# Low halves of weight blocks on GpSimd outside the recurrences, and new durations in the planner's table

## The chip, the cores and the metric

One NeuronCore of a Trainium2 chip runs the whole program. It has a matrix engine (TensorE, PE in the profile, with its weight loads as PEld), three engines for elementwise work (VectorE, DVE; ScalarE, ACT; GpSimd, POOL), a queue that issues transfers (SyncE, SP), an on-chip memory (SBUF, 128 partitions), and a small memory (PSUM) into which TensorE writes and from which VectorE and ScalarE read. Each engine takes its instructions in the order of the program and waits at an instruction until what it needs is there. The metric is device time in microseconds, from the start of the program to its end.

## The reference

A decoder trunk of two layers over 512 tokens of width 1024. Everything is computed in float32.

```python
for l in range(DEPTH):
    h = x @ w_in[l]                       # 1024 -> 10016 columns, for all branches
    y_rwkv = _rwkv7_branch(...)           # recurrence with a 64x64 state in each of 8 heads
    y_mla  = _mla_branch(...)             # causal attention, low-rank q and kv
    y_conv = _conformer_conv_branch(...)  # depthwise convolution of width 31, layer norm
    y_mem  = _memory_xattn_branch(...)    # cross-attention into 256 memory tokens
    proj   = einsum('bsnc,ncd->bsnd', branches, w_o_branch[l])
    gates  = sigmoid(merge + b_gate[l])
    merged = sum(gates * proj, axis=2)
    out    = merged @ w_out[l]
    x = _layer_norm(DEEPNORM_ALPHA * x + out, ln_g[l], ln_b[l])
```

## The kernel before

**Products in two halves.** A float32 matrix product is made of float16 ones. Each operand is split into a high half, the value rounded to float16, and a low half, what the rounding left; `mm3` issues three matmuls (high by low, high by high, low by high). The weights come as blocks of 128x1024 float32 (some 672, 640 or 768 wide), 512 KB each, into three raw buffers (tile tag `wr`, named w in the profile). `weights` spawns a task for each block: ScalarE writes the high half, scaled by 32 (`w12h` for block 12), and VectorE the low half (`w12l`) in one `scalar_tensor_tensor`: raw times 32, minus high. Both steps are in `split`. A block is as a rule split whole (`step` is the number of its parts, 2 or 3); the very first block and some of the last projection's go part by part (`step` 1). There are 236 low halves in the program. Four pairs of split blocks are held at a time, and about four parts (`LOOK`) are fetched ahead of the one that TensorE works on.

**Order.** The order of all instructions is fixed when the kernel is built, by a planner (`Plan`). It has a clock for each engine and gives every operation a duration by a table in `Engine.__getattr__`; `plan.now()` is TensorE's clock. One stream of TensorE's work (items such as a projection of 128 channels, `project`) runs as its operands become ready in the plan; tasks (attention blocks, units of the recurrence, splits of weights) step in when their time has come. A task that yields "slack" comes back when VectorE's clock in the plan has run out of work: so the 30 taps of each of the four convolutions of a layer (`taps`, tile cacc) fill VectorE's idle time. An item of the convolution's gate starts only when the convolution is through its 30 taps and its normalization (`conv_norm`, tiles ct, cn, cb, yc). What the planner takes to be short or early in error is waited for on the chip, since each engine keeps the planned order.

**Stages.** In a layer: latent projections, attention and cross-attention, with the first convolution taps (40 to 255 us in layer 0, 745 to 990 in layer 1); then the recurrence (`rwkv_unit`, eight units, from `begin_rwkv` on), into which projections, gates and merges are woven as filling for TensorE (255 to 545 and 990 to 1341); then the rest of the merges, the output projection and the layer norm. In the recurrence GpSimd inverts small triangular matrices (`substitution`, tiles ZT, W, tmpW on 32 partitions). Outside it GpSimd has only the reciprocal roots of norms (`rstd_of`, tiles lrs, rsl).

**Transfers.** All are issued by SP in order: the weight blocks, each when one of the three raw buffers is free, and between them the transposes of attention weights (mP to mPT, xP to xT) and the small transfers of the recurrence.

All operations of VectorE, ScalarE and GpSimd are recorded under one line, L285, that of the helper which calls the engine; matmuls under L370, transposes on TensorE under L375. So the rows are told apart by their tiles.

Of the kernel before, what the change touches and what calls it, by code (L numbers as in the profile page):

```python
# [17 lines left out]
ALU = mybir.AluOpType  # L18
# [17 lines left out]
WR = 3  # L36
WH = 8
WSCALE = 32.0
PROB = 16384.0
HEADS = 2  # L40
FIRST = 30
# [209 lines left out]
class Engine:  # L251
# [5 lines left out]
    def __getattr__(self, name):  # L257
        f = getattr(self.eng, name)

        def call(*a, **k):  # L260
            o = k.get("out", a[0] if a else None)
            i = k.get("in_", k.get("in0", a[1] if len(a) > 1 else o))
            n = 1
            for d in (o if name in ("activation", "copy") or self.key == "POOL" else i).shape[1:]:
                n *= d
            args = list(a) + list(k.values())
            psum = any(x.space == bass.MemoryType.PSUM for x in args if hasattr(x, "tensor"))
            regs = sum(hasattr(k.get(x), "tensor") for x in ("scale", "bias", "scalar", "scalar1", "scalar2"))
            if self.key == "ACT":
                c = (150 if psum else 115) + 0.83 * n + (150 if regs > 1 else 90 if regs or "accum_out" in k else 0)  # L270
            elif self.key == "POOL":
                c = 420 + 155 * n if k.get("op") == ALU.pow else 235 + 3.5 * n if n < 100 else 250 + 1.6 * n
            elif name == "scalar_tensor_tensor":
                c = 130 + 1.07 * n
            elif name in ("tensor_scalar", "tensor_copy"):
                c = (100 + 0.95 * n if psum else 68 + 0.53 * n) + (145 if regs else 0)
            elif name == "tensor_tensor_scan":
                c = 140 + 2.0 * n
            elif name == "bn_aggr":
                c = 66 + n  # L280
            else:
                c = 75 + 1.04 * n
            outs = _names(o, k.get("accum_out"))
            self.plan.op(self.key, c, outs, [x for x in _names(*args) if x not in outs], _banks(*args))
            return self.plan.keep(f(*a, **k))  # L285

        return call
# [60 lines left out]
def build(ctx: ExitStack, tc: tile.TileContext, A, out, log, slots, dbg=None):  # L348
    nc = tc.nc
    plan = Plan(tc.keep_in_program_order)  # L350
    V, S, G = Engine(plan, nc.vector, "DVE"), Engine(plan, nc.scalar, "ACT"), Engine(plan, nc.gpsimd, "POOL")
# [51 lines left out]
    def banks(bufs):  # L403


        if bank[0]:
            bank[0].close()
        bank[0] = ExitStack()
        bank[1] += 1
        pg.pool = bank[0].enter_context(tc.tile_pool(name=f"pg{bank[1]}", bufs=bufs, space=PSUM, reuse_waits="tile"))  # L410
        pg.bufs, pg.open = bufs, [0.0] * bufs
# [113 lines left out]
        angles.append(True)  # L525


    def split(dst_h, dst_l, src, scale=1.0):

        if scale == 1.0:  # L530
            S.copy(dst_h, src)
        else:
            S.activation(dst_h, src, AF.Copy, scale=scale)
        yield
        if scale == 1.0:
            V.tensor_tensor(out=dst_l, in0=src, in1=dst_h, op=ALU.subtract)
        else:
            V.scalar_tensor_tensor(out=dst_l, in0=src, scalar=scale, in1=dst_h, op0=ALU.mult, op1=ALU.subtract)

    def two(t):  # L540
        return t[:, 0:512], t[:, 512:1024]
# [6 lines left out]

    wlive = {"raw": 0, "hl": 0}

    whole = [1]

    def weights(name, src, parts, last=False):


        wlive["raw"] += 1
        cols = sum(parts)
        raw = wp.tile([128, 1024], F32, tag="wr", name=name, bufs=WR)[:, 0:cols]
        DMA(raw, src)
        ws = [[] for _ in parts]  # L560

        def run():
            e, n = 0, len(parts)
            step = 1 if whole[0] or last else n
            whole[0] = 0
            for a in range(0, n, step):
                c = sum(parts[a:a + step])
                if last:
                    h, lo = two(u(f"{name}{a}", 1024, F16))
                else:  # L570
                    while wlive["hl"] + step > WH:
                        yield lambda: wlive["hl"] + step <= WH
                    wlive["hl"] += step
                    h, lo = (wp.tile([128, 1024], F16, tag="w" + x, name=f"{name}{x}{a}") for x in "hl")
                h, lo = h[:, 0:c], lo[:, 0:c]
                yield from split(h, lo, raw[:, e:e + c], WSCALE)
                e += c
                f = 0
                for i in range(a, a + step):
                    ws[i].extend((h[:, f:f + parts[i]], lo[:, f:f + parts[i]]))  # L580
                    f += parts[i]
                yield
            wlive["raw"] -= 1

        plan.spawn(run(), plan.done[raw.tensor.name][0])
        return ws

# [148 lines left out]
    def layer_items(l):  # L736
# [66 lines left out]
        def begin_rwkv(get):  # L803
            yield lambda: "mla" in L
            banks(2)
            L["rp"] = open_phase(f"rp{l}")

            lh, ll, lx = ([L["rp"].tile([128, 512], F16, tag=n + x, name=n + x + t_) for x in "wa"] for n in ("lh", "ll", "lx"))
            L["lora"] = list(zip(lh, ll, lx))
            L["blk"] = [L["rp"].tile([32] + n, F32, tag=x, name=x + t_) for x, n in (("W", [16, 16]), ("ZT", [16, 16]), ("tmpW", [56]))]  # L810
            L["V"] = L["rp"].tile([128, 4, 64], F32, tag="V", name="V" + t_)
            V.tensor_copy(L["V"][:, :, 0:32], cc("id2")[:, 0:32].unsqueeze(1).to_broadcast([128, 4, 32]))
            raws = [u(f"raw{x}" + t_) for x in "wa"]
            for h in range(2):
                for half in HALF:
                    DMA(raws[h][half], A["w2a2"][l, HALF[h]])

            def parts():
                for h in range(2):
                    plan.due(raws[h])  # L820
                    yield
                    yield from split(lh[h], ll[h], raws[h])
                L["lh"] = True

            plan.spawn(parts())
# [42 lines left out]
        def rwkv_unit(j, hf, r, k, v):  # L868
# [55 lines left out]
            for cp, c2, h in quads:  # L924
                c = 2 * cp + c2
                MM(g0[HALF[c2], h, 64 * cp:64 * cp + 64], AR[HALF[h], c, 0], bt[HALF[h], 64 * c:64 * c + 64], start=True, stop=True, four=True)
            for cp, c2, h in quads:
                c = 2 * cp + c2
# [6 lines left out]
            for i, dst in enumerate((full, N)):  # L935
                V.tensor_tensor(out=by2(dst), in0=g0[:, :, 0:128].rearrange("p h (c w) -> p h c w", c=2),
                                in1=lm[:, 1 - i].unsqueeze(1).unsqueeze(1).to_broadcast([128, 2, 2, 64]), op=ALU.mult)
# [6 lines left out]
            W, ZT, tmp = L["blk"]  # L944
# [131 lines left out]
            for x, src, rhs in ((gp, bt, AR[:, :, 1]), (gv, kt, AR.rearrange("p c m w -> p c (m w)"))):  # L1076
                for cp, c2, h in quads:
                    c = 2 * cp + c2
                    MM(x[HALF[c2], h, cp], src[HALF[h], 64 * c:64 * c + 64], rhs[HALF[h], c], start=True, stop=True, four=True)
            for c2, cp, h in quads:  # L1080
# [6 lines left out]
                            in1=cc("minc").unsqueeze(1).unsqueeze(1).to_broadcast([128, 2, 2, 64]), op=ALU.mult)  # L1087
            mask = cst[:, CCOL["mstr"][0]:CCOL["minc"][1]]
            V.tensor_tensor(out=NQ.rearrange("p (h a) m w -> p h a (m w)", h=2), in0=gv,
                            in1=mask.unsqueeze(1).unsqueeze(1).to_broadcast([128, 2, 2, 128]), op=ALU.mult)  # L1090
# [30 lines left out]
            for cp in range(2):  # L1121
                for first in (True, False):
                    for c2 in range(2):
                        for h in range(2):
                            e = 2 * h + cp
                            x, y = (bk1[:, e], vt[:, e]) if first else (BP[:, e, 0:64], VA[:, 2 * (h ^ cp) + cp, 0:64])
                            MM(hh[HALF[h], c2, cp], x[HALF[c2]], y[HALF[c2]], start=first, stop=not first, four=True)
            for h in range(2):
                for first in (True, False):
                    for cp in range(2):  # L1130
                        for c2 in range(2):
                            e = 2 * h + cp
# [80 lines left out]
            if L["units"] == 8:  # L1213
                close_phase()
                banks(4)
                L["rwkv"] = True

        def room():
# [929 lines left out]
```

## Time and profile before

| | |
|---|---|
| median of 3 runs | 1455.22 us (1454.55 to 1455.3) |
| the profiled execution | 1457.4 us |
| its span, first to last instruction | 1455.6 us |
| mean granted TensorE clock | 0.985 |
| TensorE busy | 1396.6 us, 96% of the span |
| VectorE busy | 1069.8 us, 73% |
| ScalarE busy | 650.3 us, 45% |
| GpSimd busy | 242.2 us, 17% |

A row of the groups or of the timeline reads: line, engine, operation, what is written <- what is read, shapes, count; then busy microseconds and mean nanoseconds of one, or in the timeline the start and the length in front. A row of a window reads: from and to, its length, busy time and count by engine, then the granted TensorE clock, the share of the DMA engines that was busy and GB/s. Buffer numbers are left out of tiles' names.

### The profile page before, as it was taken

Reading aid. Unit: us, or ns where it says so; the run is one execution under the profiler, and the core shown is the slowest. Engines: PE = TensorE matmul, PEld = TensorE weight load, DVE = VectorE, ACT = ScalarE, POOL = GpSimd, SP = SyncE. Lnnn points to the kernel's source line nnn. Section 1 sums busy time; section 2 is a strip of 40 time slices with the busy share of each in tenths; the row PEclk is TensorE's granted clock in tenths of the full one; section 3 lists DMA queues with packets and bytes.
Section 4 is the critical chain, followed back from the end, with each engine's and each line's share of the span. In section 5 each row is a group of like instructions: output and inputs, shape, how many; then the busy total and the mean of one; then the engine's idle time right before and its main releaser. Section 6 shows DMA issues by size and latency. Waiting matters only on the chain. (4 is left out here: it accounts for less than half of the span.)

```text
span 1455.6 us, 29966 instructions
## 1 busy us (share of the span) xinstructions
PE 1396.6 (96%) x12134; PEld 754.1 (52%) x12134; DVE 1069.8 (73%) x2186; ACT 650.3 (45%) x1227; POOL 242.2 (17%) x557
## 2 busy tenths in 40 slices
PE   9999989999999789999999998999999998998997
PEld 6655544455555554444775544444455555554444
DVE  6688878888787876446654888888888868745756
ACT  5556564444443333344265556634444434432340
POOL 0000000355152600000010000000743433110001
PEclk9999999999999989999999999999999999999999
DMA  6445675231321024233443347662122221324331
GB/s 224 147 117 134 143 139 160 68 115 49 114 70 63 7 101 165 98 116 120 137 156 106 98 116 152 140 175 83 65 94 79 87 81 61 106 90 144 132 116 58
DMA packets 126539, 161.04 MB, mean 111 GB/s; under 512 B 83776, under 2 KB 85312, under 8 KB 126400
## 3 DMA queue, kind: packets, MB, share of 16 engines
q1 hardware_dynamic: 126400, 159.12, 36.6%
q8 instruction: 95, 1.56, 0.4%
q14 instruction: 44, 0.36, 0.1%
HBM read 133.39 MB, written 5.24 MB: 95 GB/s over the span
## 5 line engine op out<-in xcount | busy, mean ns | idle before, releaser
L285 DVE SCALAR_TENSOR_TENSOR cacc<-hpad,prm,cacc 128x512 f32<-128x512 f32 x240 | 179.9, 752 | 2.7
L285 ACT ACTIVATE tm<-ps_m,prm 128x512 f32<-128x512 f32 x64 | 44.0, 687 | 190.9 <-PE ps_m L370 180.2
L285 POOL TENSOR_SCALAR ZT<-W 32x256 f32<-32x256 f32 x16 | 12.2, 761 | 588.6 <-DMA W<-scr 362.5
L285 DVE SCALAR_TENSOR_TENSOR mt<-tm,po 128x512 f32<-128x512 f32 x48 | 32.9, 686 | 102.7 <-PE po L370 72.4
L285 POOL TENSOR_TENSOR ZT<-ZT,tmpW 32x14 f32<-32x14 f32 (+6 forms) x224 | 92.8, 414 | 17.6
L285 POOL TENSOR_TENSOR tmpW<-ZT,W 32x14 f32<-32x14 f32 (+6 forms) x224 | 92.3, 412 | 15.6
L370 PEld LDWEIGHTS <-mg 128*128 128x128 f16 x504 | 49.3, 98 | 34.0
L285 ACT ACTIVATE ms<-ms,nmm 128x128 f32<-128x128 f32 (+3 forms) x64 | 32.1, 501 | 18.4 <-DVE nmm L285 18.2
L285 ACT ACTIVATE mP<-ms,smm 128x128 f16<-128x128 f32 (+3 forms) x64 | 33.0, 527 | 13.5 <-issue 8.5
L370 PE MATMUL ms<-kT,qT 96*128 96x128 f16 (+3 forms) x192 | 36.3, 300 | 2.1 <-DMA kT<-xk 1.7
L285 ACT COPY Y<-gb 64x256 f32<-64x256 f32 x32 | 11.7, 367 | 57.6 <-DVE B L285 57.4
L285 POOL TENSOR_SCALAR gr<-gm 128x4 f32<-128x4 f32 x16 | 6.8, 423 | 179.0 <-DVE gm L285 179.0
L285 DVE TENSOR_TENSOR merged<-merged,mt 128x512 f32<-128x512 f32 x48 | 33.7, 703 | 1.7
L285 DVE SCALAR_TENSOR_TENSOR mP<-ms,smm,mP 128x128 f16<-128x128 f32 (+3 forms) x64 | 34.2, 544 | 0.0
L285 POOL TENSOR_SCALAR lrs<-lmv 128x1 f32<-128x1 f32 x4 | 2.2, 543 | 181.5 <-DVE lmv L285 177.3
L370 PEld LDWEIGHTS <-xh 128*128 128x128 f16 x256 | 25.0, 98 | 13.8 <-issue 2.5
L285 DVE TENSOR_REDUCE nmm<-ms 128x1 f32<-128x128 f32 (+3 forms) x64 | 30.4, 481 | 0.8 <-PE ms L370 0.2
L370 PEld LDWEIGHTS <-qT 96*128 96x128 f16 x192 | 17.1, 98 | 17.1 <-issue 3.5
L285 POOL TENSOR_TENSOR lrs<-lrs,mhalf 128x1 f32<-128x1 f32 x8 | 5.9, 742 | 107.0 <-DVE lrs L285 106.7
L285 DVE SCALAR_TENSOR_TENSOR z<-pz,z 128x256 f32<-128x256 f32 (+1 forms) x15 | 7.7, 512 | 20.9 <-PE pz L370 20.9
L285 ACT ACTIVATE mg<-merged 128x512 f16<-128x512 f32 x16 | 10.1, 630 | 28.1 <-DVE merged L285 28.1
L285 DVE SCALAR_TENSOR_TENSOR merged<-tm,po 128x512 f32<-128x512 f32 x16 | 11.0, 686 | 14.2 <-PE po L370 9.3
(1959 smaller groups left out, 4471.3 us busy)
## 6 DMA issues: line engine op xcount, KB each, us to landing
w<-in_w_ch_dram SPq DMA_DIRECT2D x146, 512.0 KB, 4.0
w<-in_w_o_dram SPq DMA_DIRECT2D x32, 512.0 KB, 3.9
w<-in_w_out_dram SPq DMA_DIRECT2D x16, 512.0 KB, 3.4
w<-in_w_lat_dram SPq DMA_DIRECT2D x16, 336.0 KB, 3.7
w<-in_w_mk_dram SPq DMA_DIRECT2D x8, 512.0 KB, 4.1
w<-in_w_mv_dram SPq DMA_DIRECT2D x8, 512.0 KB, 3.4
w<-in_w_qk_dram SPq DMA_DIRECT2D x8, 320.0 KB, 3.4
x<-in_xT_dram SPq DMA_DIRECT2D x8, 256.0 KB, 5.7
```

The lines of the kernel that those rows point to most:

```text
L285: return self.plan.keep(f(*a, **k))
L370: plan.keep(nc.tensor.matmul(o, lhsT, rhs, start=start, stop=stop))
```

## The change

Two edits in one. First, `split` gets a condition W. Where it holds, when the low half's turn comes, the low half is made by two operations on GpSimd instead of one on VectorE: the raw block is multiplied by 32 in place, and the high half is subtracted from it. For weight blocks the condition is that no recurrence is under way (`busy` holds a layer from `begin_rwkv` to the end of its eighth unit) and that the block is split whole (`step > 1`); besides, GpSimd's clock in the plan must be less than `POOLED`, 2000 ns, ahead of TensorE's. Other splits (activations, memory) stay as they were. The planner books a GpSimd operation of n elements a partition at 250 + 1.6 n ns, as before.

Second, durations of VectorE in the planner's table: a `scalar_tensor_tensor` of 1000 and more elements 1.01 instead of 1.07 ns an element; a reciprocal 165 ns (before 75 + 1.04 n); `bn_aggr` 170 + 4 n (before 66 + n); a `tensor_reduce` out of SBUF 250 + 1.04 n (before 75 + 1.04 n).

```diff
+POOLED = 2000.0
...
             elif name == "scalar_tensor_tensor":
-                c = 130 + 1.07 * n
+                c = 130 + (1.07 if n < 1000 else 1.01) * n
+            elif name == "reciprocal":
+                c = 165
...
             elif name == "bn_aggr":
-                c = 66 + n
+                c = 170 + 4 * n
+            elif name == "tensor_reduce" and not psum:
+                c = 250 + 1.04 * n
...
-    def split(dst_h, dst_l, src, scale=1.0):
+    def split(dst_h, dst_l, src, scale=1.0, W=None):
...
-            V.scalar_tensor_tensor(out=dst_l, in0=src, scalar=scale, in1=dst_h, op0=ALU.mult, op1=ALU.subtract)
+            if W and W() and plan.clk["POOL"] < plan.now() + POOLED:
+                G.tensor_scalar(out=src, in0=src, scalar1=scale, scalar2=None, op0=ALU.mult)
+                G.tensor_tensor(out=dst_l, in0=src, in1=dst_h, op=ALU.subtract)
+            else:
+                V.scalar_tensor_tensor(out=dst_l, in0=src, scalar=scale, in1=dst_h, op0=ALU.mult, op1=ALU.subtract)
...
-    whole = [1]
+    whole, busy = [1], set()
...
-                yield from split(h, lo, raw[:, e:e + c], WSCALE)
+                yield from split(h, lo, raw[:, e:e + c], WSCALE, lambda: not busy and step > 1)
...
             L["lora"] = list(zip(lh, ll, lx))
+            busy.add(l)
...
                 close_phase()
                 banks(4)
+                busy.discard(l)
                 L["rwkv"] = True
```

## The prediction

> **What bounds the kernel now.** I read the page first, for the engines' shares, then the table of windows cut at the stages, then the waits.
>
> ```profile
> span 1455.6 us, 29966 instructions
> ...
> PE 1396.6 (96%) x12134; PEld 754.1 (52%) x12134; DVE 1069.8 (73%) x2186; ACT 650.3 (45%) x1227; POOL 242.2 (17%) x557
> ```
>
> TensorE is busy 96% of the span; 59 us are idle. GpSimd (POOL) is busy 17%. The stages differ, so the next table cuts the span: the stages before the two recurrences (40 to 255 and 745 to 990), the end of the first (485 to 520), the merge that follows (545 to 745), a hole in the second (1200 to 1212), the last merge. After the length come busy time and count for PE, PEld, DVE, ACT, POOL, then the granted clock.
>
> ```profile
> 40.00:255.00 215.00, 204.63 (x1336) 112.07 (x1335) 172.43 (x366) 121.09 (x257) 2.05 (x3) 0.98 0.58 142
> 485.00:520.00 35.00, 23.01 (x659) 18.74 (x658) 26.79 (x85) 9.18 (x21) 14.62 (x43) 0.80 0.18 54
> 545.00:745.00 200.00, 199.72 (x1123) 108.09 (x1120) 106.94 (x170) 72.01 (x97) 6.77 (x10) 1.00 0.38 130
> 745.00:990.00 245.00, 232.02 (x1461) 124.39 (x1462) 191.62 (x395) 135.46 (x291) 2.05 (x3) 0.99 0.51 134
> 1200.00:1212.00 12.00, 7.17 (x246) 6.28 (x246) 7.75 (x17) 6.51 (x13) 0.00 (x0) 0.89 0.01 3
> 1341.00:1447.00 106.00, 105.98 (x504) 49.62 (x501) 67.84 (x106) 28.80 (x38) 2.83 (x3) 0.98 0.32 111
> ```
>
> In the two merges TensorE has no gap at all: work taken off VectorE there is worth nothing. In the attention stages VectorE is busy 80% (172.4 of 215) and 78%, TensorE is idle 10.4 and 13.0 us. The dearest hole is 485 to 520: 12.0 us idle, and a clock of 0.80, which costs the 23.0 busy us another 4.6. With the 4.8 us at 1200, 21.4 us can be had. The first waits for the convolution: two of its taps are still there after 485 (first row: busy time and count of the taps in that window), and its normalization then comes block by block. The second ends where the same items of layer 1 start.
>
> ```profile
> 485.00:520.00 35.00, 1.49 (x2) 0.80 0.18 54
> 517.30 1.09 PE L375 MATMUL ct<-cst,cacc 128*128 128x128 f32 x4 [1.23 <-DVE cn L285]
> ```
>
> So the change can gain only by giving VectorE time before those taps.
>
> **The change, part by part.** What leaves VectorE: the low halves, read as busy time and count of the instructions on the raw weight tile w, in 40 to 255, 545 to 745, 745 to 990 and 1341 to the end.
>
> ```profile
> 40.00:255.00 215.00, 43.12 (x37) 0.98 0.58 142
> 545.00:745.00 200.00, 48.93 (x43) 1.00 0.38 130
> 745.00:990.00 245.00, 47.49 (x43) 0.99 0.51 134
> 1341.00:1456.00 115.00, 22.08 (x21) 0.96 0.33 113
> ```
>
> That is 1.17 us a block in the first attention stage, 1.10 in the second.
>
> What it costs on POOL: a scale and a subtract over 128x1024. Neither shape stands in the trace. The nearest rows (min/median/max ns in the first two; count, busy us and mean ns in the memsets):
>
> ```profile
> L285 POOL TENSOR_SCALAR ZT<-W x16: 605/712/1124, 270.2 to 1264.7; 32x256 f32<-32x256 f32 x16
> L285 POOL TENSOR_SCALAR crs<-cmv x8: 187/192/193, 503.0 to 1198.7; 128x1 f32<-128x1 f32 x8
> L285 POOL MEMSET ZT<- 32x16 f32 x16 | 1.8, 115 | 0.9
> L285 POOL MEMSET causal<- 128x128 bf16 x1 | 0.2, 204 | 0.3 <-POOLq L2140 0.3
> 423.71 0.20 POOL L285 TENSOR_TENSOR ZT<-ZT,tmpW 32x14 f32<-32x14 f32 x1
> 434.82 0.28 POOL L285 TENSOR_TENSOR ZT<-ZT,tmpW 32x56 f32<-32x56 f32 x1
> ```
>
> Scale: (605-192)/255 = 1.62 ns an element, so 1.85 us for 1024; by the memsets' slope, 0.8 ns, 0.92 at least. Subtract: 0.08 us for 42 elements, 1.9 ns each, 2.1 us; with the 10 ns that the rows round, up to 2.6. The pair takes 4.0 us (3.0 to 4.5) where VectorE takes 1.2. I take 4.0, since the scale is the same kind of instruction as the first row. The planner books 2 x 1.89. POOL then has 37 x 4.0 = 148 of 215 us to do: it fits.
>
> What the two engines do to each other decides the sign. In time order, start and length:
>
> ```profile
> 295.33 1.22 DVE L285 SCALAR_TENSOR_TENSOR w54l<-w,w54h 128x1024 f16<-128x1024 f32 x1
> 295.01 0.29 POOL L285 TENSOR_TENSOR tmpW<-ZT,W 32x50 f32<-32x50 f32 x1
> 295.38 1.30 POOL L285 TENSOR_TENSOR ZT<-ZT,tmpW 32x50 f32<-32x50 f32 x1
> 399.48 0.61 POOL L285 TENSOR_SCALAR ZT<-W 32x256 f32<-32x256 f32 x1 [10.13 <-DMA W<-scr]
> 399.48 1.15 DVE L285 TENSOR_TENSOR merged<-merged,mt 128x512 f32<-128x512 f32 x1
> L285 DVE TENSOR_TENSOR merged<-merged,mt 128x512 f32<-128x512 f32 x48 | 33.7, 703 | 1.7
> 423.49 0.68 DVE L285 SCALAR_TENSOR_TENSOR mt<-tm,po 128x512 f32<-128x512 f32 x1
> ```
>
> A POOL operation that starts while VectorE reads two SBUF tiles (w54l) takes 1.30 instead of 0.29: it waits until VectorE is through. The other way round, merged takes 1.15 instead of 0.70: it waited 0.45 of the 0.61 that POOL ran. Beside mt, which reads one of its tiles from PSUM, POOL keeps its 0.20. So a POOL operation shuts out VectorE's operations on two SBUF tiles for all but its last 0.15 us: 1.70 + 1.95 = 3.65 us a block. The taps are such operations:
>
> ```profile
> 40.00:255.00 215.00, 40.95 (x56) 0.98 0.58 142
> 745.00:990.00 245.00, 51.08 (x70) 0.99 0.51 134
> L285 DVE SCALAR_TENSOR_TENSOR cacc<-hpad,prm,cacc 128x512 f32<-128x512 f32 x53 | 39.4, 745 | 0.7
> ```
>
> One tap every 3.8 us, if spread at random, loses hold - 3.8 x (1 - exp(-hold/3.8)): 0.33 + 0.43 = 0.75 us a block. But taps are let in where VectorE would idle, hence come in runs (idle before 53 of them: 0.7 us together), and xy, v, mo, the rotary products read two SBUF tiles too; every POOL operation meeting one at its start would be 3.65. I take 1.6, nearer the first. VectorE then gains 1.17 and loses 1.6 a block. Its program is written for the gain: it falls behind by 37 x 1.6 = 59 us, against 42.6 us idle: 16.6 over, of which I charge TensorE half, since late taps hold nobody up for long: **+8** (-10, all the idle time there, to +35, from 2.1 a block). Second layer: 43 x 1.5 = 64.5 against 53.4, half of 11: **+5** (-12 to +28).
>
> No run here shows a hold longer than 0.61 us. The Trainium skill (SBUF — State Buffer, "Who interferes with whom") says that whoever starts first keeps the shared pair for the whole instruction; by that rule the sum stays as it is. If a long POOL operation gave the port up in between, a block would lose at most two waits of 0.45 us, and the first rival below is the case.
>
> Low halves come later. Two places, then the points where TensorE now waits for a low half (us in total, times, longest):
>
> ```profile
> 587.28 1.22 DVE L285 SCALAR_TENSOR_TENSOR w94l<-w,w94h 128x1024 f16<-128x1024 f32 x1
> L370 PEld LDWEIGHTS <-w94l x8: 98/98/98, 593.7 to 598.2; 128*128 128x128 f16 x8
> PE pmv L370 <- DVE w126l L285: 1.9, 1, 1.9
> PE ps_val L370 <- DVE w11l L285: 1.1, 1, 1.1
> PE pl L370 <- DVE w2l L285: 0.6, 1, 0.6
> ```
>
> In the merge w94l is ready 5.2 us before its use: 2.8 us more are hidden, as long as POOL keeps up: 43 x 4.0 = 172 of 200 us. At w126, w11 and w2 nothing hides them. w2 is 672 wide, 0.66 of a block: 2.6 us instead of 0.8, **+1.5** at the start (0 to 3.5; the wait for w11h at 45 may swallow it). The others, and POOL running behind where blocks come every 4 us (680 to 745): **+4** (0 to 20). The raw tile is kept some 3 us longer; SP's next load waits for it, and so do the transposes behind it on SP: inside the +35.
>
> POOL's other work queues behind the pairs. At the layer's end that is the norm's rstd, on the way to the next layer's input:
>
> ```profile
> 732.49 1.03 POOL L285 TENSOR_SCALAR lrs<-lmv 128x1 f32<-128x1 f32 x1 [177.29 <-DVE lmv L285]
> ```
>
> Four of them, each behind up to 4 us: **+2** (0 to 8); memory projections cover the rest.
>
> The convolution's hole: the planned order has taps earlier, the real VectorE does not get them done sooner. I take a third of 21.4: **-7** (-22 to 0).
>
> The planner's durations: +89 ns a reciprocal, +122 a bn_aggr, +175 an SBUF reduce, -61 a wide low half. Against the rows (mean ns last)
>
> ```profile
> L285 DVE RECIPROCAL smm<-smm 128x1 f32<-128x1 f32 x64 | 10.5, 164 | 2.2
> L285 DVE BATCH_NORM_AGGREGATE gm<-gs 128x2 f32<-128x6 f32 x64 | 5.8, 153 | 0.0
> L285 DVE TENSOR_REDUCE Mc<-Md 128x64 f32<-128x256 f32 x16 | 9.2, 576 | 0.0
> ```
>
> they come nearer (165, 194, 516). They shift the order, a few us of VectorE a layer: **0** (-3 to 3).
>
> Sum: 8 + 5 + 1.5 + 4 + 2 - 7 = +13.5 on the profiled execution's 1457.4: 1470.9. The median of the runs, 1455.2, lies 2.2 below that execution, so 1468.7, **1469**.
>
> **Rivals.** First, faster: the relief is real. It decides from a loss of 1.15 us a block downward, as with taps alone at random (0.75) or a port given back. Then taps are through earlier, the holes at 485 and 1200 close (-21.4), less the start and the low halves (+5.5): 1441.5, timed 1439. For it: only 80% of VectorE's time is used, and PSUM readers run freely beside POOL. Against it: the rows at 295 and 399.
>
> Second, nothing to see: all stays within TensorE's full stages, or the rule lets few blocks through: 1455. Against the latter: the planner has POOL 3.9 us ahead after a pair and lets the next in under 2, while blocks come every 4.7 to 5.8 us.
>
> Third, POOL becomes the bound of the merges. At 4.5 and two waits of 0.4 behind VectorE, a pair takes 5.3 us: 43 x 5.3 = 228 for 200 us, less 5 of cover, +23; the last merge 21 x 5.3 = 111 for 106, +5. With the other terms (+9.5): 1495, timed 1493.
>
> **How the numbers follow.** The forecast has 0.46, with 1458.5 to 1485 its own range; faster 0.30; nothing 0.12; POOL-bound 0.12. A measurement tells about 0.2% (2.9 us) from no change. Faster 0.31, within 0.12, slower 0.57. The range, 1438 to 1495, reaches into both outer cases and leaves out 0.18.
>
> **What would show it.** POOL some 150 pairs, 550 to 600 us busier, scale near 1.85 and subtract near 2.1 us at their shortest; taps of 2 us and more beside them (0.745 on average now); VectorE's busy time in the attention stages not lower by 43 and 47 us but about level; TensorE idle more than 10.4 and 13.0 us there, less than 12 at the first hole. I am wrong if taps keep 0.75 us beside a running subtract, or if the last tap of layer 0 comes well before 499 with the attention stage no longer.

## The result and the profile after

The changed kernel takes 1538.22 us (median of 4 runs, 1534.42 to 1539.57) against 1455.26 beside it: ratio 1.0568, 95% interval 1.0548 to 1.0588. It is slower, as forecast, by 83 us instead of 14.

The page of the changed kernel, its head and engines, and the groups that the prediction turned on. (In this kernel the engines' line is L290, matmuls are L375, transposes L380.)

```profile
span 1537.8 us, 30362 instructions
...
PE 1417.9 (92%) x12134; PEld 755.7 (49%) x12134; DVE 1065.9 (69%) x2060; ACT 653.9 (43%) x1227; POOL 845.6 (55%) x809
...
L290 POOL TENSOR_SCALAR w<-w 128x1024 f32<-128x1024 f32 (+3 forms) x126 | 348.1, 2763 | 173.2 <-ACT w152h L290 20.3
...
L290 DVE SCALAR_TENSOR_TENSOR cacc<-hpad,prm,cacc 128x512 f32<-128x512 f32 x240 | 245.0, 1023 | 3.6
```

TensorE's idle time went from 59.0 to 119.9 us, +60.9. Its busy time for the same 12134 matmuls went from 1396.6 to 1417.9, +21.3: the mean granted clock fell from 0.985 to 0.971. Together that is the 82.2 us between the spans. VectorE lost 126 instructions and hardly any busy time (1069.8 to 1065.9). A low half cost it 1.12 us (161.62 us for 144 in the prediction's four windows), 141 for 126; so the rest of its work became 137 us longer, 1.09 us for each block that GpSimd took. The taps show it: 1.02 us on average, 0.75 before.

Windows of the changed kernel: first attention stage, the former hole, the rest of the first merge, second attention stage, last merge; columns as before.

```profile
40.00:280.00 240.00, 206.51 (x1307) 111.30 (x1305) 194.91 (x360) 123.12 (x267) 178.09 (x76) 0.96 0.50 121
485.00:520.00 35.00, 35.00 (x315) 17.76 (x306) 27.50 (x60) 13.72 (x23) 13.38 (x32) 1.00 0.30 97
652.00:794.00 142.00, 126.68 (x740) 73.39 (x739) 54.65 (x84) 43.15 (x56) 117.97 (x54) 0.97 0.30 106
802.00:1077.00 275.00, 244.80 (x1459) 126.72 (x1459) 201.92 (x374) 138.93 (x294) 197.53 (x88) 0.94 0.43 114
1416.00:1529.00 113.00, 106.85 (x503) 49.44 (x501) 68.52 (x90) 28.69 (x38) 81.05 (x33) 0.98 0.30 104
```

The hole at 485 is gone: TensorE is full there and at full clock. But the merges, without a gap before, have 15.3 and 6.2 us of them, and the attention stages 33.5 and 30.2 (10.4 and 13.0 before). By stage, from the trace (the recurrence counted from the first write of its tile V to its last yr; the next layer's input by its first transpose):

| stage | before | after | with GpSimd in the attention stages only |
|---|---|---|---|
| start to first recurrence | 250.5 | 280.6 | 280.0 |
| recurrence and merge of layer 0 | 492.9 | 513.7 | 491.8 |
| to second recurrence | 246.3 | 283.0 | 281.0 |
| second recurrence | 351.5 | 338.9 | 338.9 |
| last merge, to the end | 114.3 | 121.6 | 114.2 |

The two recurrences alone, to the last yr, first before, then in the changed kernel:

```profile
250.50:624.20 373.70, 361.24 (x3976) 191.43 (x3975) 281.41 (x588) 148.33 (x267) 115.57 (x264) 0.98 0.26 86
989.80:1341.30 351.50, 340.67 (x3901) 182.03 (x3899) 265.15 (x570) 145.75 (x263) 113.65 (x264) 0.99 0.26 84
```

```profile
280.60:654.30 373.70, 364.93 (x4006) 191.11 (x4004) 268.25 (x562) 156.08 (x277) 121.99 (x267) 0.98 0.28 90
1077.30:1416.20 338.90, 331.54 (x3871) 177.56 (x3870) 248.87 (x544) 140.82 (x256) 111.69 (x265) 0.99 0.27 87
```

With as many matmuls as before (7877), the two together are 12.6 us shorter: TensorE is 7.1 us less idle and 5.4 less busy. The first, with 30 more matmuls than before, is as long as it was; the second is shorter.

What TensorE waited for in the changed kernel (us in total, times, longest):

```profile
PE ty L380 <- DVE yb L290: 8.5, 2, 5.0
PE pq L375 <- ACT w152h L290: 6.8, 1, 6.8
PE ps_val L375 <- POOL w11l L290: 4.3, 1, 4.3
PE ps_m L375 <- POOL w162l L290: 3.9, 1, 3.9
PE pl L375 <- POOL w1l L290: 3.6, 1, 3.6
PE pz L375 <- POOL w118l L290: 3.5, 1, 3.5
PE pz L375 <- POOL w123l L290: 3.5, 1, 3.5
PE pmv L375 <- POOL w126l L290: 3.4, 1, 3.4
```

In all, 32 rows of this view name a low half on GpSimd; they add up to 63 us, none over 4.3. Before, VectorE's low halves held TensorE up for 4.7 us. The loss is not one stall; it is many short ones. A low half comes later for two reasons: the pair is longer than VectorE's one operation, and it queues behind the pair before it. In the first merge, start and length:

```profile
742.45 1.05 ACT L290 ACTIVATE w118h<-w 128x1024 f16<-128x1024 f32 x1
743.99 2.77 POOL L290 TENSOR_SCALAR w<-w 128x1024 f32<-128x1024 f32 x1
746.83 2.12 POOL L290 TENSOR_TENSOR w117l<-w,w117h 128x1024 f16<-128x1024 f32 x1
748.92 2.77 POOL L290 TENSOR_SCALAR w<-w 128x1024 f32<-128x1024 f32 x1
751.77 2.12 POOL L290 TENSOR_TENSOR w118l<-w,w118h 128x1024 f16<-128x1024 f32 x1
```

The high half of w118 is ready at 743.50; its pair starts 5.4 us later, behind that of w117, and TensorE waits 3.5 us. Of the 126 pairs, 61 start more than 2 us after their high half is ready. For these 126 blocks the low half follows the high half by 6.5 us at the median; it was 1.7 before.

### The profile page after: what moved, and what is told of

The parts are those of the page before. It is cut to its first block, busy times and chain, and to the rows that moved or that the text cites. A ratio compares the mean times of both kernels' runs of the same rounds, so it can differ in the third digit from the quotient of the medians.

```text
span 1537.8 us, 30362 instructions
## 1 busy us (share of the span) xinstructions
PE 1417.9 (92%) x12134; PEld 755.7 (49%) x12134; DVE 1065.9 (69%) x2060; ACT 653.9 (43%) x1227; POOL 845.6 (55%) x809
## 5 line engine op out<-in xcount | busy, mean ns | idle before, releaser
L290 POOL TENSOR_SCALAR w<-w 128x1024 f32<-128x1024 f32 (+3 forms) x126 | 348.1, 2763 | 173.2 <-ACT w152h L290 20.3
L290 DVE SCALAR_TENSOR_TENSOR cacc<-hpad,prm,cacc 128x512 f32<-128x512 f32 x240 | 245.0, 1023 | 3.6
L290 POOL TENSOR_SCALAR gr<-gm 128x4 f32<-128x4 f32 x16 | 7.0, 438 | 234.5 <-DVE gm L290 234.5
L290 POOL TENSOR_SCALAR ZT<-W 32x256 f32<-32x256 f32 x16 | 11.0, 688 | 169.6 <-DMA W<-scr 142.6
L290 DVE SCALAR_TENSOR_TENSOR mt<-tm,po 128x512 f32<-128x512 f32 x48 | 32.8, 684 | 102.2 <-PE po L375 98.8
L290 POOL TENSOR_TENSOR ZT<-ZT,tmpW 32x14 f32<-32x14 f32 (+6 forms) x224 | 92.4, 413 | 17.6
L290 ACT ACTIVATE tm<-ps_m,prm 128x512 f32<-128x512 f32 x64 | 44.0, 687 | 136.2 <-PE ps_m L375 136.1
L290 POOL TENSOR_TENSOR tmpW<-ZT,W 32x14 f32<-32x14 f32 (+6 forms) x224 | 92.4, 413 | 15.8
L375 PEld LDWEIGHTS <-mg 128*128 128x128 f16 x504 | 50.0, 99 | 51.7 <-issue 17.5
L290 ACT ACTIVATE ms<-ms,nmm 128x128 f32<-128x128 f32 (+3 forms) x64 | 32.0, 500 | 36.1 <-DVE nmm L290 35.7
L290 DVE TENSOR_TENSOR merged<-merged,mt 128x512 f32<-128x512 f32 x48 | 38.9, 810 | 1.7
L375 PE MATMUL ms<-kT,qT 96*128 96x128 f16 (+3 forms) x192 | 37.4, 312 | 1.7 <-DVE smx L290 1.4
L290 ACT ACTIVATE mP<-ms,smm 128x128 f16<-128x128 f32 (+3 forms) x64 | 33.2, 527 | 9.3 <-ACT ms L290 4.6
L375 PEld LDWEIGHTS <-xh 128*128 128x128 f16 x256 | 25.6, 100 | 18.4 <-issue 6.3
L290 DVE TENSOR_REDUCE nmm<-ms 128x1 f32<-128x128 f32 (+3 forms) x64 | 30.1, 479 | 6.4 <-PE ms L375 6.3
L290 DVE SCALAR_TENSOR_TENSOR mP<-ms,smm,mP 128x128 f16<-128x128 f32 (+3 forms) x64 | 34.3, 543 | 0.4 <-ACT ms L290 0.3
L290 DVE SCALAR_TENSOR_TENSOR z<-pz,z 128x256 f32<-128x256 f32 (+1 forms) x15 | 7.7, 510 | 32.6 <-PE pz L375 32.6
L290 ACT COPY Y<-gb 64x256 f32<-64x256 f32 x32 | 11.7, 367 | 39.1 <-DVE B L290 33.7
L375 PEld LDWEIGHTS <-qT 96*128 96x128 f16 x192 | 17.2, 100 | 16.6 <-issue 2.0
L290 ACT COPY VA<-va 128x512 f32<-128x512 f32 x16 | 9.4, 585 | 37.4 <-PE va L375 29.2
L290 ACT ACTIVATE mg<-merged 128x512 f16<-128x512 f32 x16 | 10.0, 628 | 34.0 <-DVE merged L290 34.0
L290 ACT CAST rbh<-w 128x256 fp32r<-128x256 f32 x16 | 6.5, 404 | 40.6 <-DVE w L290 40.5
```

Of the source, the lines that this page charges most:

```text
L375: plan.keep(nc.tensor.matmul(o, lhsT, rhs, start=start, stop=stop))
```

## Experiments

Three theories to begin with. **Lateness**: the low halves come late because GpSimd's two operations take 4.9 us. **Shutting out**: VectorE, held off while GpSimd works, falls behind and TensorE waits for VectorE. **Order**: the planner's new durations give a worse order. Each run stands beside runs of the kernel before, 1455 to 1457 us.

**Durations alone.** The edits of the durations stay; the condition that gives low halves to GpSimd is never true.

```diff
-            if W and W() and plan.clk["POOL"] < plan.now() + POOLED:
+            if False:
```

> The new durations of VectorE alone; all low halves stay on VectorE. Theory 1 (late low halves: GpSimd takes 4.9 us for a pair that the planner books at 3.9, and TensorE waits): 1450 to 1460 us, no wait of TensorE for GpSimd. Theory 2 (VectorE is shut out of the port): the same. Theory 3 (the new order that the durations give is the cost): over 1480 us.

1476.55 us, 1.0137 (1.0122 to 1.0152): +20.5 us from edits that the forecast had at nothing.

**GpSimd alone.** The changed kernel with the durations taken back.

```diff
-                c = 130 + (1.07 if n < 1000 else 1.01) * n
+                c = 130 + 1.07 * n
...
-            elif name == "reciprocal":
-                c = 165
```

> Low halves on GpSimd as in the changed kernel, with the old durations. Theories 1 and 2: 1525 to 1550 us, TensorE waiting some 60 us for GpSimd's low halves. Theory 3: under 1500 us.

1521.91 us, 1.0449 (1.0434 to 1.0465): +66. The two parts nearly add up to the whole, 20.5 + 66 against 83.

**A planner that knows the cost.** The planner books what the trace showed for the two wide operations.

```diff
+                if n > 600:
+                    c = 200 + 2.51 * n if name == "tensor_scalar" else 110 + 1.97 * n
```

> The changed kernel, but the planner books the scale at 200 + 2.51 n ns and the subtract at 110 + 1.97 n, as the profile of the changed kernel has them (2.77 and 2.12 us for 1024), so fewer blocks go to GpSimd and the order allows for them. Theory 1, the plan's error alone: 1450 to 1480 us, waits for GpSimd's low halves under 15 us. Theory 1 with GpSimd simply too slow whatever the plan knows, or theory 2: over 1500 us. Theory 3: over 1520 us.

1529.07 us, 1.0507 (1.048 to 1.0533). TensorE's waits for GpSimd's low halves fall from 63 to 49 us, those for VectorE rise from 34 to 45. This plan, with 118 pairs in place of 126, orders around the slow pair only a little: 9 us.

**Without the scale.** The scale is left out, so the low halves hold other numbers; the other operations stay.

```diff
-                G.tensor_scalar(out=src, in0=src, scalar1=scale, scalar2=None, op0=ALU.mult)
```

> The changed kernel without the scale on GpSimd: the low half is raw minus high, so the numbers that come out are others; the subtract is booked at 1.89 us and takes 2.1. Theory 1: the waits for low halves nearly go, 1435 to 1465 us. Theory 2: half of the shutting out stays, 1485 to 1505 us. Theory 3: over 1520 us.

1480.88 us, 1.0169 (1.0149 to 1.0189): 57 us less, only 4 above the durations alone. Waits for GpSimd's low halves: 4 us. So in this order nearly all of GpSimd's cost comes with the scale; the subtract, with VectorE relieved of the whole low half, is almost paid for.

**Why the scale is slow.** Behind the last item of the kernel before stand GpSimd operations on scratch tiles.

```diff
+                plan.keep(nc.gpsimd.tensor_scalar(out=x, in0=x, scalar1=1.0, scalar2=None, op0=ALU.mult))
+                plan.keep(nc.gpsimd.tensor_scalar(out=x, in0=y, scalar1=1.0, scalar2=None, op0=ALU.mult))
+                plan.keep(nc.gpsimd.tensor_scalar(out=x, in0=y, scalar1=1.0, scalar2=0.0, op0=ALU.mult, op1=ALU.add))
+                plan.keep(nc.gpsimd.tensor_copy(x, y))
...
```

> The kernel before, with 72 GpSimd operations on scratch tiles behind its last item: six forms at 256, 512 and 1024 columns on 128 and on 32 partitions (multiply by a number in place, the same from another tile, the same with an addition, a copy, a product of two tiles, a subtraction of f16 from f32), each twice. After showed the scale at 2.77 us for 1024 columns on 128 partitions where the forecast had 1.85 from a row of 32x256. If it is the form (in place), the multiply from another tile takes near 1.85 us and the one in place 2.77. If it is the partitions, 32 partitions give 1.85 and 128 give 2.77 in either form. If neither, both forms take 2.77 on 32 and on 128 partitions, 0.84 at 256 columns, and the row of 0.605 at 32x256 was a special one.

The groups of that run (da, dc are f32 tiles, db is f16; L2051 multiplies in place, L2052 from another tile, L2053 multiplies and adds zero; mean ns behind the busy time):

```profile
L2051 POOL TENSOR_SCALAR da<-da 128x1024 f32<-128x1024 f32 x2 | 5.5, 2767 | 0.2
L2051 POOL TENSOR_SCALAR da<-da 32x1024 f32<-32x1024 f32 x2 | 5.5, 2758 | 0.2
L2052 POOL TENSOR_SCALAR da<-dc 128x1024 f32<-128x1024 f32 x2 | 5.5, 2768 | 0.2
L2053 POOL TENSOR_SCALAR da<-dc 128x1024 f32<-128x1024 f32 x2 | 2.1, 1044 | 0.2
L2054 POOL COPY da<-dc 128x1024 f32<-128x1024 f32 x2 | 2.1, 1036 | 0.1
L2056 POOL TENSOR_TENSOR db<-da,db 128x1024 f16<-128x1024 f32 x2 | 4.2, 2119 | 0.2
L2053 POOL TENSOR_SCALAR da<-dc 32x256 f32<-32x256 f32 x2 | 0.8, 394 | 0.2
```

Neither the place nor the partitions matter: the multiply alone takes 2.77 us, the multiply with an addition 1.04, as long as a copy. The last row has the size and the form of the ZT row that the forecast scaled from (there 0.605 us, with a transposed read). The third answer that the expectation offered had the figures, both forms slow on 32 as on 128 partitions and the row of ZT a special one. What makes it special, which no answer had, is the number of operations in the instruction.

**GpSimd beside, on tiles of its own.** The kernel before in its order; at the points where the changed kernel gives a block to GpSimd, a scale and a subtract of 128x1024 run on scratch, 121 pairs. Each stands behind a read of 8 columns of the block's high half (not shown), which sets the pace.

```diff
+                plan.keep(nc.gpsimd.tensor_scalar(out=da, in0=da, scalar1=1.0, scalar2=None, op0=ALU.mult))
+                plan.keep(nc.gpsimd.tensor_tensor(out=db, in0=da, in1=db, op=ALU.subtract))
```

> The kernel before in its own order, every low half still on VectorE and on time; GpSimd does a scale and a subtract of 128x1024 on scratch tiles of its own at the same points and as often as in the changed kernel, so only what the two engines do to each other is added. If the low halves' lateness is what costs the 66 us (theory 1), this costs little: VectorE is held up in the attention stages and TensorE waits for it some 5 to 20 us longer, 1460 to 1475 us, and the merges stay free of gaps. If holding up VectorE is what costs them (theory 2), it comes out at 1505 or more, since VectorE has all its former work beside it.

1570.04 us, 1.079 (1.0766 to 1.0814): +113, far above what lateness allows, and in the range that shutting out had. VectorE is busy for 1240.5 us instead of 1069.8, with the same work.

**The same with fills.** Five fills in place of the two.

```diff
+                plan.keep(nc.gpsimd.memset(da, 1.0))
```

> As the run with scratch reads beside, but GpSimd only writes: five fills of 128x1024 at each point, about as long as the pair. If it is reading two SBUF tiles on the one side and GpSimd's access of any kind on the other that exclude each other, taps reach 1 us and more again and the time is that of the run with reads. If a fill takes nothing from VectorE, taps keep 0.72 to 0.75 us and the time is 1455 within 4 us.

1481.71 us, 1.0173 (1.0158 to 1.0189). Neither expectation holds. Taps keep their length, as the second one said; the time does not. From the view by tile (min/median/max ns), first before, then with scratch reads, then with fills:

```profile
L285 DVE SCALAR_TENSOR_TENSOR cacc<-hpad,prm,cacc x240: 718/747/1105, 63.0 to 1169.2; 128x512 f32<-128x512 f32 x120
L285 DVE TENSOR_SCALAR latq<-latq,rsl x8: 410/416/421, 45.5 to 791.5; 128x384 f32<-128x384 f32 x8
```

```profile
L285 DVE SCALAR_TENSOR_TENSOR cacc<-hpad,prm,cacc x240: 719/747/2710, 81.3 to 1280.6; 128x512 f32<-128x512 f32 x120
```

```profile
L285 DVE SCALAR_TENSOR_TENSOR cacc<-hpad,prm,cacc x240: 721/746/1178, 73.2 to 1193.7; 128x512 f32<-128x512 f32 x120
L285 DVE TENSOR_SCALAR latq<-latq,rsl x8: 850/1181/1289, 51.9 to 813.2; 128x384 f32<-128x384 f32 x8
```

Fills leave the taps alone and hold up VectorE's operations on a single f32 tile instead (latq 1.18 us for 0.42). And they stand in GpSimd's queue ahead of rsl, the root for which latq and latk wait:

```profile
49.61 0.20 POOL L285 TENSOR_TENSOR rsl<-ssl,cst 128x8 f32<-128x8 f32 x1
...
51.89 3.49 DVE L285 TENSOR_SCALAR latq<-latq,rsl 128x384 f32<-128x384 f32 x3 [7.13 <-POOL rsl L285]
...
58.70 0.61 PE L370 MATMUL ps_val<-xh,w11l 128*128 128x512 f16 x1 [10.23 <-DVE w11l L285]
```

VectorE sits 7.13 us in front of latq, w11l stands behind it on VectorE, and TensorE waits 10.23 us for w11l. In the changed kernel VectorE's wait at that place was 3.21 us. GpSimd is busy for 865 us with fills and for 958 with the pairs, so the 88 us between the two times go mostly with what GpSimd does and less with how long. They are no clean price of the reading, since the fills have waits of their own.

**The scale on ScalarE**, in place, with the durations of before.

```diff
-                G.tensor_scalar(out=src, in0=src, scalar1=scale, scalar2=None, op0=ALU.mult)
+                S.activation(src, src, AF.Copy, scale=scale)
```

> The changed low halves with the scale on ScalarE in place (some 1.0 us there) and only the subtract on GpSimd, the full computation, and the planner's durations as before the change. Theory 1 (the pair's 4.9 us make the low halves late): GpSimd's part is 2.1 us and its gaps at TensorE fall from 58 to under 12 us, the time is 1450 to 1472. Theory 2 (VectorE shut out): the subtract still shuts out VectorE for 2 us a block, above 1480. ScalarE has room (45% busy), so a third way, ScalarE's high halves late by the scale in front of them, is 10 us at most.

1483.26 us, 1.0177 (1.0152 to 1.0203): above lateness' range, where shutting out had it. Its waits for GpSimd are small (15 us, for 58), as lateness had it; those for VectorE are 38 (24 in the run with GpSimd alone). The subtract with the scale elsewhere stands 26 us above the kernel before here, and stood 4 above the durations alone in the run without the scale; the orders differ too, so its own price stays open.

**The fast form of the scale.** Two operations in the instruction.

```diff
-                G.tensor_scalar(out=src, in0=src, scalar1=scale, scalar2=None, op0=ALU.mult)
+                G.tensor_scalar(out=src, in0=src, scalar1=scale, scalar2=0.0, op0=ALU.mult, op1=ALU.add)
```

> The changed kernel with its scale written with two operations (times 32, plus 0) in one instruction; the run of the forms showed 1.04 us for it at 128x1024 against 2.77 us with the one operation, so the pair falls from 4.9 to 3.2 us and nothing else is edited. Theory 1 (what the pair's length costs): TensorE's gaps behind GpSimd's low halves fall from 63 to 10 to 25 us and the time lies at 1485 to 1505, near the run without the scale (1481). Theory 2 (what VectorE loses while it is shut out): VectorE's loss falls with the time that GpSimd works, by a third, but its gaps stay at 35 to 45 us, and the time stays above 1505. If the form is slow for another reason than its one operation, the scale stays at 2.7 us and the time at 1538.

1517.41 us, 1.0408 (1.0385 to 1.043). The page of this run:

```profile
PE 1406.7 (93%) x12134; PEld 754.1 (50%) x12134; DVE 1085.5 (72%) x2060; ACT 651.7 (43%) x1227; POOL 650.9 (43%) x809
...
L290 POOL TENSOR_SCALAR w<-w 128x1024 f32<-128x1024 f32 (+3 forms) x126 | 142.8, 1133 | 327.1 <-ACT w152h L290 21.8
...
L290 DVE SCALAR_TENSOR_TENSOR cacc<-hpad,prm,cacc 128x512 f32<-128x512 f32 x240 | 249.0, 1040 | 3.6
```

GpSimd is 195 us less busy, and waits for its low halves fall from 63 to 15.5 us, as lateness predicted. But waits for VectorE rise from 34 to 69: the time is shutting out's. VectorE is no better off with the short scale, 1085.5 us busy for 1065.9. The trace of the changed kernel says why. In order of time, start and length:

```profile
258.83 2.94 POOL L290 TENSOR_SCALAR w<-w 128x1024 f32<-128x1024 f32 x1 [4.56 <-ACT w41h L290]
259.06 1.52 DVE L290 SCALAR_TENSOR_TENSOR cacc<-hpad,prm,cacc 128x512 f32<-128x512 f32 x1
260.50 0.74 DVE L290 SCALAR_TENSOR_TENSOR cacc<-hpad,prm,cacc 128x512 f32<-128x512 f32 x1
261.17 0.74 DVE L290 SCALAR_TENSOR_TENSOR cacc<-hpad,prm,cacc 128x512 f32<-128x512 f32 x1
261.85 2.13 POOL L290 TENSOR_TENSOR w41l<-w,w41h 128x1024 f16<-128x1024 f32 x1
261.94 2.58 DVE L290 SCALAR_TENSOR_TENSOR cacc<-hpad,prm,cacc 128x512 f32<-128x512 f32 x1
```

A tap that starts with the subtract ends at 264.52, 0.54 us after it: it is let in some 0.2 us before the subtract's end, after 1.9 us. The tap that starts with the slow scale ends at 260.58, 1.19 us *before* the scale's end, and the two after it run at full speed inside the scale. Every tap of this trace that starts in the first 0.8 us of a wide scale (22 taps) ends so, 1.19 us ahead of it; so 1.19 and the tap's own 0.75 us of the 2.77 are left when VectorE is let in: the slow form keeps VectorE out for 0.83 us and works alone for the rest. In the fast form the taps end 0.54 us behind the scale, hence are let in after 0.83 of its 1.04 us too. The forms differ in length, not in how long one of them keeps VectorE out. Why the waits for VectorE doubled with holds of the same length, and passed the 35 to 45 us that shutting out had, is not shown.

**The fast form with the durations of before.** Both edits above together.

> The same with the planner's durations as they were before the change. If the durations' 20 us add to the rest as they did with the slow scale, 1465 to 1485. If VectorE's waits are the larger part by now, as in the run with the scale on ScalarE (1483 with these durations), not below 1480.

1499.17 us, 1.0284 (1.0262 to 1.0306): outside the first range, above the second bound. Waits: 21 us for GpSimd's low halves, 46 for VectorE.

**The durations one by one, and edits without meaning.** The kernel before with a part of the new durations, or with the constant of one formula 4 ns up or down:

```diff
-                c = 130 + 1.07 * n
+                c = 134 + 1.07 * n
```

> The kernel before with two of the new durations alone, reciprocal and bn_aggr, which stand 128 times in the recurrences. All four durations together cost 20.5 us (1476.5), in the second recurrence. If it is these two (they make the planner put less beside the recurrence's chain on VectorE), 1470 to 1480 with the last taps of layer 1 near 1224; if the order merely falls out one way or another with any edit of a duration (no one cause), it is as likely 1450 as 1470, and the wide one alone moves the time as well.

> The kernel before with one new duration alone, that of the operations over 1000 columns wide (the low halves), 61 ns shorter by the plan. If reciprocal and bn_aggr carry the 20 us, this stays at 1455 within 4 us. If any edit of a duration lets the order fall out differently, it moves by 5 us or more either way.

> The kernel before with one new duration alone, that of a reduction of an SBUF tile (+175 ns by the plan, 16 in each recurrence). The first three single edits gave +9.6 us (the two norms) and -13.4 us (the wide one), all four together +20.5. If each duration has an effect of its own and these add, this one is +24 us, 1480. If the order falls out one way or another with any edit, it lies anywhere between 1443 and 1477, and nearer 1455 than 1480.

> The kernel before with a duration changed without meaning: the planner books 4 ns more for each operation with a scalar and two tiles (134 for 130 in its constant, where they take 280 to 1220 ns). If the order is chosen well and true durations matter, the time stays at 1455 within 3 us. If the order falls out one way or another with any edit, it moves by more than 5 us, either way.

> The same the other way, 126 for 130. As above: within 3 us of 1455, or off by more than 5, with a sign that need not be the opposite one.

| edit of the kernel before | us | ratio (95%) |
|---|---|---|
| reciprocal and bn_aggr | 1466.61 | 1.0062 (1.004 to 1.0084) |
| the wide scalar_tensor_tensor | 1443.59 | 0.9908 (0.9888 to 0.9929) |
| reduction from SBUF | 1449.66 | 0.995 (0.9932 to 0.9968) |
| 4 ns more, without meaning | 1449.79 | 0.995 (0.9935 to 0.9965) |
| 4 ns less, without meaning | 1443.71 | 0.9909 (0.9893 to 0.9924) |
| all four new durations | 1476.55 | 1.0137 (1.0122 to 1.0152) |

The single ones sum to -11 us where all together give +20.5: they do not add, and 4 ns either way make the kernel faster. The order falls out differently with any edit, over 33 us. All the new durations together are one such draw, not a price. Four of these versions beat both kernels, with no work moved, the wide one and the 4 ns less by 13 us. Where the last one wins can be seen at the two places where a layer's convolution ends. Before, then 4 ns less:

```profile
480.00:530.00 50.00, 38.01 (x751) 25.65 (x749) 38.27 (x115) 16.11 (x36) 20.66 (x55) 0.83 0.17 51
1160.00:1215.00 55.00, 50.17 (x768) 30.36 (x767) 39.57 (x96) 20.80 (x41) 15.95 (x42) 0.95 0.19 62
```

```profile
460.00:510.00 50.00, 41.97 (x780) 28.39 (x782) 38.12 (x106) 16.73 (x38) 25.60 (x70) 0.90 0.13 38
1150.00:1205.00 55.00, 53.38 (x784) 31.14 (x782) 43.48 (x104) 19.16 (x37) 19.48 (x48) 1.00 0.22 72
```

7.2 us less idle and more clock there, with the taps of layer 0 through at 471 instead of 500.

**GpSimd in the attention stages only** (`att` holds in them, and in no merge).

```diff
-                yield from split(h, lo, raw[:, e:e + c], WSCALE, lambda: not busy and step > 1)
+                yield from split(h, lo, raw[:, e:e + c], WSCALE, lambda: att and step > 1)
```

> The changed kernel, with GpSimd taking low halves in the two attention stages and none in the merges, which go back to VectorE. TensorE's gaps behind GpSimd's low halves were 63 us, by place some 40 in the attention stages and 24 in the two merges. If the gaps of the two places are separate costs, 40 us of them stay and the time is 1505 to 1520. If GpSimd's falling behind in one stage is what makes the next late, the attention stages alone cost less: below 1500. If the merges' part is hidden anyway behind the earlier convolution, 1530 or more.

1508.4 us, 1.0361 (1.0335 to 1.0387), as two separate costs would have it: the merges cost 30 us, the rest of the change 53. Its merge windows show no gap; the second row is the last merge:

```profile
648.00:772.00 124.00, 124.00 (x746) 73.27 (x744) 68.12 (x109) 43.88 (x59) 4.51 (x8) 0.98 0.36 122
1392.00:1497.00 105.00, 105.00 (x502) 49.44 (x500) 67.02 (x104) 28.80 (x38) 2.96 (x3) 0.98 0.33 111
```

**The changed kernel with the meaningless edits.**

```diff
-                c = 130 + (1.07 if n < 1000 else 1.01) * n
+                c = 134 + (1.07 if n < 1000 else 1.01) * n
```

> The changed kernel with the same meaningless 4 ns more a booking. Five other orders of the kernel before came out between 1443.6 and 1476.6 us. If the 83 us of the change are GpSimd's work and not the order, this stays at 1520 to 1555, far above every order without it; if the order has a part in them like the one that it has in the kernel before, it moves by 5 to 20 us; if most of the 83 us were the order, it can fall under 1500.

> The same with 4 ns less a booking: 1520 to 1555 if it is GpSimd's work, under 1500 if it were mostly the order.

1539.02 us, 1.0568 (1.0551 to 1.0586), and 1536.13, 1.0559 (1.0538 to 1.0581). The change's cost is no accident of the order: its three orders with these durations lie within 3 us, 60 us above the slowest of seven orders without it.

## Why the prediction was wrong

The sign was right, the time was not: 1538 lies 43 us above the range. Step by step:

- **What leaves VectorE**, 1.17 and 1.10 us a block: as read.
- **The pair's price** fell at "I take 4.0, since the scale is the same kind of instruction as the first row". It is not: the row ZT<-W stands for an instruction with two operations (times 1, plus 0), the scale has one. On the same sizes the one form takes 2.77, the other 1.04 us. The subtract was right (2.12 us for 2.1). The pair is 4.9 us, above the bound of 4.5. A look at the operation's arguments, not only at its name and shape, would have shown that the row was of another form; not that the other form was slower.
- **The shutting out** was read rightly in kind, from the rows at 295 and 399, and too long by the scale: 0.83 + 1.9 = 2.7 us a pair instead of 3.65. The charge of 1.6 us a block measured 1.09. The Trainium skill (SBUF — State Buffer, "Who interferes with whom") calls the shared pair an exclusive lock and, for VectorE's two-port modes, has it last for the whole instruction; the subtract bears that out but for its last 0.2 us, the slow scale does not (0.83 of 2.77 us). That fills leave two-tile operations alone (0.746 us) and hold up others (latq) agrees with the same section. VectorE came out level, as the prediction's marks said (busy for 80% of the first attention stage before and 81% after). The **+8** and **+5** rested on VectorE's backlog. TensorE's waits for VectorE from the start to the first recurrence rose from 4.2 to 13.2 us, near the +8; before the second recurrence they fell from 7.0 to 3.3. TensorE's gaps in the two attention stages are 23 and 17 us larger, and mostly for another reason, the next one.
- **Low halves late, +4 (0 to 20)**, is the step that failed most: 63 us of waits in 32 places instead of 4.7. I looked at one block with cover (5.2 us in a merge) and at three without, and took the rest of the 126 for covered. At 32 places TensorE's cover was smaller than what a low half came later, 4.7 us at the median. That is more than the 3.7 us by which the pair is longer than VectorE's operation, since many pairs queue on GpSimd: 18 of the 32 waits, 29 of the 63 us, are for blocks whose pair started over 0.5 us late. The prediction named this ("POOL running behind"), for one stretch of 65 us, with a pair of 4.0 us instead of 4.9. Leaving the scale out took these waits to 4 us, and nearly all of GpSimd's cost with them.
- How much of that scale's 57 us is lateness alone? The fast form makes the pair 1.7 us shorter at the same hold: 21 us (23 with the durations of before). Its waits for VectorE are 69 us, and it still stands 60 us above the kernel before, so shutting out takes over much of what lateness gives up. The other 36 go only with the operation itself, which adds a hold of 0.83 us and a last 1.04 us of length; these two the runs do not part.
- **The queue of POOL, +2**: I counted lrs and not rsl, which stands behind low halves too (waits on VectorE of 3.2 us in layer 0 and 6.3 in layer 1, for 1.6 and 4.5 before). Its share of the 83 us was not measured by itself.
- **The convolution's hole, -7**: "the planned order has taps earlier, the real VectorE does not get them done sooner" is wrong. Layer 0's last tap ended at 404.6 instead of 500.2, and TensorE is full from 485 to 520. The gain is there, 12.6 us in the two recurrences, and not the whole 21.4, since other gaps took the hole's place: 8.8 us in the first recurrence, for 12.5 with the hole. It is smaller than what is lost to get it.
- **The durations, 0 (-3 to 3)**: +20.5. The reading that they come nearer to the rows was right and beside the point. Any edit re-deals the order, over -13 to +20 us here; no row of the trace of before could tell which.

The rivals: the **first** (faster) named its own condition, a loss under 1.15 us a block. It was met, with 1.09, and the first hole closed as it said; yet the recurrences gained 12.6 us and not 21.4, and the kernel was slower: VectorE's balance was not what decided. The **second** did not happen. The **third**, GpSimd as the bound of the merges, had 28 us for them; 29.8 were measured by taking GpSimd out there, beside and not instead of the other losses. Its mechanism holds in part: GpSimd is busy 83% of the first merge (117.97 of 142 us), and TensorE waits block by block; from 723 to 759 us, w118's pair among them, pair follows pair without a gap, and there GpSimd is the bound. Of the marks, GpSimd's extra time (603 us, just above the 600), the taps of over 2 us and the idle attention stages came as said; the scale's 1.85 us did not, and the pairs were 126 and not some 150. Layer 0's last tap came well before 499, but with the attention stage 30 us longer, so that sign of being wrong was not met as written.

The sum, +13.5, lacked 69 us of the 82.2. What it had too small: the waits for low halves (4 for 63), the durations (0 for 20.5), and TensorE's clock, which had no term but the hole's and took 21. What it had too dear: VectorE's loss (1.6 us a block for 1.09) and the hole (a gain of 7 for 12.6). These overlap, since one gap of TensorE can have two engines late behind it, and do not sum to 69.

## What to carry to other kernels

When work moves to a slower engine, the first question is not whether that engine has time but how late each result comes, by its own length and by the queue in front of it, and what cover every consumer has: list all of them, since here short waits in 32 places add up to 63 us. Price an instruction by a row of the very same form, down to how many operations it holds, and time the form by itself if there is no such row. Where a planner fixes the order, try an edit without meaning first: here 4 ns moved the time by 7 and 13 us, far more than the measurement's uncertainty, so a change of order has to beat that spread, and a few such draws can be worth more than the change.

## What the hardware showed unasked

- GpSimd multiplies a 128x1024 f32 tile by a number in 2.77 us, multiplies and adds zero in 1.04, copies in 1.04, and subtracts two tiles in 2.12; 32 partitions take as long as 128.
- The slow multiply keeps VectorE's two-tile operations out for 0.83 us only, and the fast one for as long; the subtract for 1.9 of 2.1.
- Fills by GpSimd do not touch VectorE's two-tile f32 operations (taps 0.746 us at the median; the 79 that run beside nothing else of GpSimd's than fills take 0.753 at most) and make its one-tile f32 operations wait (latq 0.42 to 1.18 us).
- The granted clock is lower where TensorE has gaps: 0.83 in the 50 us around the first hole before, 0.90 where that hole is 4 us smaller, 1.00 where it is gone. Over the whole kernel it goes from 0.985 to 0.971, and TensorE's busy time for the same matmuls grows by 21 of the 82 us.
